# A hybrid decoder layer on one core: blocks of half-array products, ranks from backward schedules, a fixed opening and one engine for the norm

## The chip, the cores and the metric

The kernel runs on one core of one Trainium2 chip. The metric is the device time of one execution in microseconds (us); the figure compared is the median over several executions. The engines are called as in the profile: PE is TensorE (matmuls), PEld its weight loads, DVE is VectorE, ACT is ScalarE, POOL is GpSimd, and SP issues most of the DMA transfers.

## The reference

One pre-norm layer of a hybrid autoregressive decoder is computed for 1024 tokens of width 1024, in fp32:

```python
h = rms_norm(x, norm_in_g)
p = h @ w_in                                   # one projection for all three head groups
y_rwkv = rwkv7_group(p_rwkv, ...)              # 8 heads x 64, a delta-rule state scanned over time
y_nsa  = nsa_group(p_nsa, ...)                 # 4 heads: compressed, selected and window attention
kv = rms_norm(mem, mem_norm_g) @ w_mem_kv      # 256 memory tokens
y_mem  = memory_group(p_mem, mem_k, mem_v)     # 4 heads of cross-attention
x = x + concat(y_rwkv, y_nsa, y_mem) @ w_out
return rms_norm(x, norm_final_g)
```

With 16 blocks of 64 tokens and a top 16 of blocks, the selected branch attends to every block up to the token's own.

## The kernel before, in words

**Tiles.** The eight 128-token tiles of `x` are normed (`normed`), transposed on PE against an identity (`transposed`, lines 633 to 640) and kept as a high and a low fp32r half in two `H` tiles (`hT`). Every projection (`proj`) streams 512 columns of `hT` through a 128x128 weight tile three times (high x high, high x low, low x high); a weight tile is loaded into `wr`, rounded by ACT into `wh` and subtracted by POOL or DVE into `wl` (`split`, lines 569 to 571).

**Norm of a tile.** `normed` squares the tile on ACT (line 622), makes the factor on POOL (lines 623 and 566, into the small tile `ss`, of which there are two), and multiplies by factor and gain: POOL takes the first `X_POOL` = 192 columns in two multiplications (lines 627 and 628), DVE the other 832 in one (line 630). It is called for the eight tiles of `x` and, later, the two of `mem`.

**RWKV.** After the projections, `elementwise` (lines 868 to 949) prepares each pair of heads on DVE, ACT and POOL. `inverse` solves the 32x32 triangular systems: 31 steps of two DVE instructions each (lines 761 and 762), then a way through DRAM (`md`, `nd`, `st_d`) and 32x32 products on PE. There are two inverses, each for two pairs of heads. When both are through, `chunk` advances the state over 16 chunks of 64 tokens, one after the other, with products of 64 rows or 64 columns.

**Half-array products.** A product whose stationary operand has at most 64 (or 32) rows or columns uses a part of the 128x128 array; `_mode` gives its form as (rows, columns), each rounded up to 32, 64 or 128. They are emitted in groups without anything between them: 16, 8, 8 and 8 of them in a chunk, 32 in each of the four product steps of an inverse, 8 in each half of `elementwise`, 16 or 32 in the compression. An fp32 product shows as two matmul records in the trace.

**The order.** Every stage is a generator; `flow` interleaves them with ranks and latencies written by hand, and so emits one sequence of instructions. `ordered` then replaces this sequence. It reads the instructions, derives their dependences (`_depend`) and the reuse of buffers (`_slots`), and simulates the five engines with costs of its own (`_schedule`): whenever an engine is free, it takes of the instructions that are ready the one with the highest rank. The rank of an instruction is the length of the longest path of work behind it (`tail`), with engines taken as unlimited. PE lowers the rank of a candidate of another form than the last by `SWITCH` = 300 (ns). This is done in `ROUNDS` = 4 rounds, each from the order of the one before, and the order with the earliest simulated end is pinned on each engine:

```python
for a, b in zip(line, line[1:]):
    tc.add_manual_dep(ops[b].i, ops[a].i.name, ..., reason="order")
```

So each engine has one fixed order on the chip, and an instruction that isn't ready holds up all behind it on its engine.

Of the kernel before, what the change touches and what calls it, by code (L numbers as in the profile page):

```python
# [79 lines left out]
L_LAST = 1.41  # L80
L_W = 2.38
X_W = 1
X_POOL = 192
L_XW = 0.42
E_POOL = 1
E_KV = 0
# [194 lines left out]
def _depend(ops):  # L281

    past, bank = {}, {}
    for o in ops:
        o.data, o.same = set(), set()
        for t, parts in o.reads:
            for q, m in parts.items():
                for e in past.get((t.name, q), ()):
                    if e[0] & m and (e[2] or t.space == PSUM and ops[e[1]].e != o.e):
                        o.data.add(e[1])  # L290
        for t, parts in o.writes:
            for q, m in parts.items():
                keep = []
                for e in past.get((t.name, q), ()):
                    if e[0] & m:
                        o.data.add(e[1])
                        e = (e[0] & ~m, e[1], e[2])
                    if e[0]:
                        keep.append(e)
                keep.append((m, o.k, True))  # L300
                past[t.name, q] = keep
        for t, parts in o.reads:
            for q, m in parts.items():
                past.setdefault((t.name, q), []).append((m, o.k, False))
        if o.e == "PE":
            t = o.writes[0][0].name
            if t in bank:
                o.same.add(bank[t])
            bank[t] = o.k
        o.data.discard(o.k)  # L310
        if o.e == "PE":
            o.same |= {p for p in o.data if ops[p].e == "PE"}
            o.data -= o.same
# [29 lines left out]
    return took, late  # L343


def _schedule(ops, users, tags, took, phase, rank=None):
    n = len(ops)
    preds = [None] * n
    for o in ops:
        preds[o.k] = {p: 0 for p in o.data}  # L350
        for p in o.same:
            preds[o.k][p] = 1
    for names in tags.values():
        for a, b in zip(names, names[1:]):
            p = users[a][0]
            for k in users[b]:
                if k != p and any(w[0].name == b for w in ops[k].writes):
                    preds[k].setdefault(p, 2)
    for t, old in took.items():

        for k in users[t]:
            if any(w[0].name == t for w in ops[k].writes):
                for p in users[old]:
                    if p != k:
                        preds[k][p] = 1 if ops[k].e == "PE" and ops[p].e == "PE" else 0
    for o in ops:
        o.preds = preds[o.k]
    succ = [[] for _ in range(n)]
    for k in range(n):
        for p, same in preds[k].items():  # L370
            succ[p].append((k, same))

    deg = [len(s) for s in succ]
    tail = [0.0] * n
    stack = [k for k in range(n) if not deg[k]]
    seen = 0
    while stack:
        k = stack.pop()
        seen += 1
        o = ops[k]  # L380
        t = o.took
        for s, same in succ[k]:
            t = max(t, (0.0 if same == 2 else o.occ if same else o.took + LAG[ops[s].e]) + tail[s])
        tail[k] = t
        for p in preds[k]:
            deg[p] -= 1
            if not deg[p]:
                stack.append(p)
    assert seen == n, "a circle"
    if rank is not None:  # L390
        tail = [tail[k] + rank(ops[k]) for k in range(n)]
    indeg = [len(p) for p in preds]
    ready = [700.0] * n
    engines = ("PE", "DVE", "Activation", "Pool", "SP")
    free = dict.fromkeys(engines, 700.0)
    wait = {e: [] for e in engines}
    able = {e: [] for e in engines}
    order = {e: [] for e in engines}
    start = [0.0] * n
    for o in ops:  # L400
        if not indeg[o.k]:
            heapq.heappush(wait[o.e], (ready[o.k], o.k))
    lanes, port, holder, server = [0.0] * LANES, 0.0, "", 0.0
    slow, busy, prev, pe_at, pe_occ = True, 0.0, None, 0.0, 0.0
    done, end = 0, 0.0
    while done < n:
        best = None
        for e in engines:
            w, a = wait[e], able[e]
            while w and w[0][0] <= free[e]:  # L410
                k = heapq.heappop(w)[1]
                heapq.heappush(a, (-tail[k], k))
            at = free[e] if a else w[0][0] if w else None
            if at is not None and (best is None or at < best[0]):
                best = at, e
        at, e = best
        if not able[e]:
            free[e] = at
            continue
        if e == "PE" and prev is not None and len(able[e]) > 1:  # L420
            a = able[e]
            m = _mode(prev)
            k = min(a, key=lambda x: (x[0] + SWITCH * (_mode(ops[x[1]].shape) != m), x[1]))
            a.remove(k)
            heapq.heapify(a)
            k = k[1]
        else:
            k = heapq.heappop(able[e])[1]
        o = ops[k]
        s = at  # L430
        if e == "PE":

            if prev is not None and _mode(o.shape) != _mode(prev) and s < pe_at + pe_occ + 100:
                s = max(s, pe_at + pe_occ + 100 * (1 + slow))
            if prev is not None:
                a1 = min(s, pe_at + pe_occ)
                w0 = int((pe_at + phase) // WINDOW)
                e1 = (w0 + 1) * WINDOW - phase
                busy += min(a1, e1) - pe_at
                w1 = int((s + phase) // WINDOW)  # L440
                if w1 > w0:
                    slow = busy < 0.5 * WINDOW or slow and busy < 0.8 * WINDOW
                    busy = max(0.0, a1 - e1)
                    if w1 > w0 + 1:
                        slow, busy = slow or busy < 0.5 * WINDOW or w1 > w0 + 2, 0.0
            pe_at, prev = s, o.shape
            pe_occ = o.occ * (1 + slow)
            free[e] = s + pe_occ
            f = s + o.took * (1.5 if slow else 1.0)
        elif o.dma:  # L450
            issue, l0, serve, l1 = o.dma
            lane = min(range(LANES), key=lambda x: lanes[x])
            s = max(s, lanes[lane])
            server = max(server, s + issue + l0) + serve
            f = server + l1
            lanes[lane] = f
            free[e] = s + o.occ
        else:
            t, c = o.took, o.occ
            if o.lock:  # L460
                x = max(0.0, port - s) if holder != e else 0.0
                t, c, port, holder = t + x, c + x, s + t + x - 30, e
            f = s + t
            free[e] = s + c
        start[k] = s
        order[e].append(k)
        done += 1
        end = max(end, f)
        for x, same in succ[k]:
            ready[x] = max(ready[x], s if same == 2 else free[e] if same else f + LAG[ops[x].e])  # L470
            indeg[x] -= 1
            if not indeg[x]:
                heapq.heappush(wait[ops[x].e], (ready[x], x))
    return order, start, end


SWITCH = 300.0
BUFS = {"A_a": N_A, "C_a": 2, "P4_p4": N_P4, "NP_p4": N_NP, "S2_s2": N_S2, "N2_s2": N_N2, "T2_s2": N_T2, "H_h": 2, "wr_w": N_WR,
        "wl_w": 2, "wh_w": 2, "pa_ps": 6, "ch_ps": 2, "ss_small": 2, "edge_small": 2, "n8_small": 2, "ost_small": 2, "mst_small": 4,
        "cst_small": 1, "st_small": 2, "wst_small": 3, "xe_small": 1, "sgc_small": 1, "md_dram": 2, "nd_dram": 2}  # L480
ROUNDS = 4


def ordered(nc, tc, log=None):
    ops = _read(list(nc.cur_bb.bb.instructions))
    _depend(ops)
    users, tags = _tiles(ops)
    seq = list(range(len(ops)))
    best = None
    for n in range(ROUNDS):  # L490
        took, late = _slots(users, tags, seq)
        order, start, end = _schedule(ops, users, tags, took, 1100.0)
        if log is not None:
            log(n, late, end)
        if best is None or end < best[0]:
            best = end, order
        seq = sorted(range(len(ops)), key=lambda k: (start[k], k))
    end, order = best
    for e, line in order.items():
        for a, b in zip(line, line[1:]):  # L500
            tc.add_manual_dep(ops[b].i, ops[a].i.name, mybir.DependencyInfo(mybir.DependencyClass.NoSync, mybir.DependencyReason.DATA), reason="order")
# [1337 lines left out]
```

## Time and profile before

| | |
|---|---|
| median of three runs | 833.57 us (832.88 to 837.31) |
| profiled execution, its own time | 830.76 us |
| its span, first to last instruction | 829.0 us |
| mean granted TensorE clock | 0.968 |
| PE busy | 768.8 us, 93% of the span |
| PEld, DVE, ACT, POOL busy | 620.0, 537.3, 386.6, 362.0 us |
| HBM | 126 GB/s over the span |

The span is what the profiler sees of the program's instructions; the execution's own time is 1.8 us longer, and the median of the timed runs is 2.8 us above that execution. Busy time of PE is the union of its matmuls, whose ends are modelled, so a busy PE may still advance slowly: at a low clock, or between two products of different forms. The granted clock tells the first, start-to-start distances of consecutive matmuls the second.

### The profile page before, as it was taken

What the parts mean: (1) busy time and instruction counts of PE and PEld (TensorE: products, weight loads), DVE (VectorE), ACT (ScalarE), POOL (GpSimd) and SP (SyncE); (2) the same over time, 40 slices, a digit from 0 to 9 for tenths busy, and PEclk for the clock granted to TensorE, in tenths of its full rate; (3) what the DMA queues carried; (4) which work ended last, traced back from release to release, by engine and by line L of the source; (5) the groups of instructions that cost most, each with busy time, mean ns of one, the idle gap of its engine ahead of it and who ended that gap; (6) DMA issues with size and microseconds to landing.
All of it is one profiled execution on the core that took longest, in us unless ns stands there. A gap on an engine that the chain in (4) does not pass through costs nothing.

```text
span 829.0 us, 15125 instructions
## 1 busy us (share of the span) xinstructions
PE 768.8 (93%) x5738; PEld 620.0 (75%) x5738; DVE 537.3 (65%) x1044; ACT 386.6 (47%) x854; POOL 362.0 (44%) x390
## 2 busy tenths in 40 slices
PE   1999999999897799899999999999998999999996
PEld 0978778787676578678787667776787988888884
DVE  4753647749987529734578786646978776776542
ACT  4542516244153113333377653435477756665541
POOL 5644716346145010513446356625424153255664
PEclk9999899999988699999999999999999999999998
DMA  8011444665437992697556575632424020221121
GB/s 339 27 44 34 138 90 132 161 158 147 114 77 202 186 202 91 172 178 211 168 173 204 167 254 182 205 96 84 127 92 157 8 66 19 71 77 51 52 84 57
DMA packets 124745, 105.67 MB, mean 127 GB/s; under 512 B 50817, under 2 KB 108545, under 8 KB 122497
## 3 DMA queue, kind: packets, MB, share of 16 engines
q1 hardware_dynamic: 108096, 95.57, 41.4%
q10 hardware_dynamic: 16576, 9.14, 4.2%
q8 instruction: 45, 0.74, 0.3%
q14 instruction: 28, 0.22, 0.1%
HBM read 68.52 MB, written 36.18 MB: 126 GB/s over the span
## 4 chain that ended last, share of the span: by engine, by line
PE 71%; DVE 12%; DMA 6%; ACT 4%; issue 3%; POOL 3%; SPq 1%; ACTq 0%; DVEq 0%; POOLq 0%
PE pa L545 42%; PE ch L545 21%; PE pa L1571 3%; DVE P L761 2%; POOL wl L571 2%; DVE A L762 2%; DMA A<-st_d 1%; DMA wr<-in_w_in_dram 1%; DMA pv<-in_pv_dram 1%; DMA g_d<-T 1%; PE pa L1154 1%; PE pa L1603 1%; ACT wh L570 1%; DMA C<-st_d 1%; DVE C L942 1%
## 5 line engine op out<-in xcount | busy, mean ns | idle before, releaser
L545 PE MATMUL pa<-H,wh 128*128 128x512 f32 (+1 forms) x928 | 294.8, 406 | 1.3 <-ACT H L639 0.8
L545 PEld LDWEIGHTS pa<-H,wh 128*128 128x128 f32 x928 | 174.6, 195 | 38.2 <-issue 3.1
L545 PE MATMUL pa<-H,wl 128*128 128x512 f32 (+1 forms) x464 | 170.7, 400 | 0.0
L571 POOL TENSOR_TENSOR wl<-wr,wh 128x1024 fp32r<-128x1024 f32 x27 | 67.6, 2503 | 100.9 <-ACT wh L570 86.2
L545 PE MATMUL ch<-H,C 128*128 128x512 f32 x360 | 109.9, 410 | 0.6 <-DVE P L1691 0.5
L545 PEld LDWEIGHTS pa<-H,wl 128*128 128x128 f32 x464 | 89.3, 193 | 16.9 <-issue 0.7
L545 PE MATMUL pa<-A 128*128 128x256 f32 (+4 forms) x416 | 87.6, 313 | 4.4 <-DVE A L925 2.0
L570 ACT ACTIVATE wh<-wr 128x1024 fp32r<-128x1024 f32 x32 | 33.9, 1058 | 103.6 <-PE pa L545 82.9
L545 PEld LDWEIGHTS ch<-H,C 128*128 128x128 f32 x360 | 63.9, 189 | 10.2 <-DVE P L1691 0.9
L545 PEld LDWEIGHTS pa<-A 128*128 128x128 f32 (+1 forms) x416 | 55.1, 173 | 14.4 <-issue 3.8
L1531 DVE TENSOR_REDUCE wst<-pa 128x1 f32<-128x384 f32 (+3 forms) x96 | 46.5, 518 | 20.8 <-PE pa L545 20.4
L545 PEld LDWEIGHTS ch<-T,C 128*64 128x64 f32 (+1 forms) x1008 | 39.3, 136 | 22.9 <-issue 8.1
L545 PE MATMUL ch<-T,C 128*64 128x64 f32 (+1 forms) x1008 | 51.8, 231 | 4.0 <-issue 1.5
L1106 DVE TENSOR_TENSOR N<-pa,S 128x512 fp32r<-128x512 f32 (+1 forms) x76 | 45.3, 614 | 9.1 <-ACT S L1105 4.3
L1105 ACT ACTIVATE S<-pa 128x512 fp32r<-128x512 f32 (+1 forms) x76 | 39.7, 546 | 14.5 <-PE pa L1571 13.3
L1541 ACT ACTIVATE NP<-pa,wst 128x384 f32<-128x384 f32 (+3 forms) x52 | 29.0, 566 | 28.8 <-DVE wst L1537 18.1
L1428 DVE SCALAR_TENSOR_TENSOR T<-ch,gc,sgc 64x64 f32<-64x64 f32 x120 | 33.9, 283 | 11.7 <-PE ch L545 5.2
L761 DVE TENSOR_TENSOR P<-A 128x31 f32<-128x31 f32 (+15 forms) x62 | 31.2, 504 | 10.7 <-DMA g_d<-T 9.5
L545 PE MATMUL ch<-N,A 128*128 128x256 f32 x132 | 35.5, 320 | 1.4 <-DVE N L1106 1.4
L545 PE MATMUL ch<-S,A 128*128 128x256 f32 x132 | 35.3, 317 | 1.1 <-ACT T L1584 1.1
L1612 POOL TENSOR_TENSOR S<-S,N 128x512 f32<-128x512 f32 x8 | 10.3, 1287 | 59.2 <-DVE N L1611 52.0
L1410 POOL TENSOR_TENSOR sgc<-T,gc 64x256 f32<-64x256 f32 x30 | 20.4, 680 | 35.8 <-DVE T L1428 34.6
(277 smaller groups left out, 1587.6 us busy)
## 6 DMA issues: line engine op xcount, KB each, us to landing
C<-st_d SPq DMA_DIRECT2D x16, 1024.0 KB, 6.1
wr<-in_w_in_dram SPq DMA_DIRECT2D x28, 512.0 KB, 3.9
st_d<-C SPq DMA_DIRECT2D x32, 256.0 KB, 4.0
st_d<-A SPq DMA_DIRECT2D x24, 256.0 KB, 4.4
A<-in_x_dram SPq DMA_DIRECT2D x8, 512.0 KB, 7.8
st_d<-NP SPq DMA_DIRECT2D x8, 512.0 KB, 3.4
P<-in_x_dram SPq DMA_DIRECT2D x8, 512.0 KB, 3.5
out_dram<-P SPq DMA_DIRECT2D x7, 512.0 KB, 2.6
```

What stands on the lines that cost most here:

```text
L545: PE.matmul(o, l, r, start=start, stop=stop, skip_group_check=True, **k)
L570: S.activation(hi, src, AF.Copy)
L571: E.tensor_sub(lo, src, hi.bitcast(F32))
L761: V.tensor_mul(t3, mt[:, 0:n, s:s + 1].to_broadcast([128, n, m]), lt[:, s:s + 1, s + 1:].to_broadcast([128, n, m]))
L762: V.tensor_add(mt[:, 0:n, s + 1:], mt[:, 0:n, s + 1:], t3)
L1105: S.activation(th[:, 0:w], psum_t, AF.Copy)
L1106: V.tensor_sub(tl_[:, 0:w], psum_t, th[:, 0:w].bitcast(F32))
L1410: G.tensor_mul(sgc[r], sv[r, q], gcb[r])
L1428: V.scalar_tensor_tensor(svn[r, q, hp, :], pn[r, hp, :], g1[r, hp], sgc[r, hp, :], op0=OP.mult, op1=OP.add)
L1531: V.tensor_reduce(st[:, 3 + a, hh:hh + 1], sc[:, 0:cw], axis=AX.X, op=OP.max, negate=True)
L1541: S.activation(p[:, c0:c0 + cw], sc[:, 0:cw], AF.Exp, bias=m, accum_out=acc)
L1571: PE.transpose(pt[:, (2 * jj + hh) * 128:(2 * jj + hh + 1) * 128], ptl[hh][:, (j + jj) * 128:(j + jj + 1) * 128], ident)
```

## The change

Four things change, none of them in what is computed.

- `X_POOL` becomes 0: the two POOL multiplications of `normed` go, and DVE's one instruction covers all 1024 columns.
- Consecutive PE instructions of one form other than (128, 128) become a block of up to 32, which `_forward` issues without anything between; all that any member waits for is asked of the first. `SWITCH` becomes 700.
- The rank comes from `_backward`: the same list scheduling from the end of the program to its start, with one instruction at a time on each engine and the start times of the last round to choose by. An instruction's rank is its distance from the end in that schedule. There are 10 rounds in place of 4. The simulated clock counts products of 32 rows as half busy and those of 64 rows as 0.85.
- The first `FIRST` = 250 instructions of the emitted sequence get their rank raised, by 1000 for each place they stand ahead of the 250th, so that they keep about the order in which they were emitted.

Besides, two reads of one PSUM tile by the same engine now keep their order (`_depend`).

```diff
-X_POOL = 192
+X_POOL = 0
@@ _depend
-                    if e[0] & m and (e[2] or t.space == PSUM and ops[e[1]].e != o.e):
-                        o.data.add(e[1])
+                    if e[0] & m and (e[2] or t.space == PSUM):
+                        (o.data if e[2] or ops[e[1]].e != o.e else o.same).add(e[1])
@@ _edges (new; its first part is that of _schedule)
+    after, head = {}, list(range(len(ops)))
+    for a, b in zip(ops, ops[1:]):
+        if a.e == b.e == "PE" and _mode(a.shape) == _mode(b.shape) != (128, 128) and len(block(head, a.k, after)) < BLOCK:
+            after[a.k] = b.k
+            head[b.k] = head[a.k]
+    for k in range(len(ops)):
+        h = head[k]
+        if h != k:
+            for p, same in preds[k].items():
+                if head[p] != h:
+                    preds[h][p] = min(same, preds[h].get(p, 2))
@@ _backward (new), the core
+        k = heapq.heappop(able[e])[1]
+        o = ops[k]
+        R[k] = max(floor[k], at + o.occ)
+        free[e] = at + o.occ
+        for p, same in preds[k].items():
+            q = ops[p]
+            d = 0.0 if same == 2 else q.occ if same else q.took + LAG[o.e] + MARGIN
+            floor[p] = max(floor[p], R[k] + d)
@@ _forward (was _schedule)
+        if forced is not None:
+            k, e, at = forced, "PE", free["PE"]
...
         if e == "PE":
+            forced = after.get(k)
...
-                busy += min(a1, e1) - pe_at
+                share = 0.5 if prev[1] == 32 else 0.85 if prev[1] == 64 else 1.0
+                busy += (min(a1, e1) - pe_at) * share
@@ constants
-SWITCH = 300.0
+MARGIN = 0.0
+FIRST = 250
+BLOCK = 32
+SWITCH = 700.0
-ROUNDS = 4
+ROUNDS = 10
@@ ordered
-        order, start, end = _schedule(ops, users, tags, took, 1100.0)
+        preds, after = _edges(ops, users, tags, took)
+        rank = _backward(ops, preds, start)
+        rank = [r + max(0.0, FIRST - k) * 1e3 for k, r in enumerate(rank)]
+        order, start, end = _forward(ops, preds, after, rank, 1100.0)
```

## Rows read from the trace of the kernel before

**Rows 1.** The page: the span and the busy time of the engines.

```profile
span 829.0 us, 15125 instructions
PE 768.8 (93%) x5738; PEld 620.0 (75%) x5738; DVE 537.3 (65%) x1044; ACT 386.6 (47%) x854; POOL 362.0 (44%) x390
```

**Rows 2.** Windows by stage: stretch, length, busy (x instructions), clock, DMA share, GB/s.

```profile
42.46:220.00 177.54, 173.19 (x888) 138.44 (x887) 112.86 (x155) 66.37 (x101) 84.17 (x84) 0.98 0.46 114
220.00:380.00 160.00, 141.36 (x1109) 113.08 (x1108) 105.98 (x199) 49.92 (x76) 40.98 (x47) 0.88 0.69 155
380.00:545.00 165.00, 161.15 (x1749) 120.90 (x1747) 112.27 (x269) 90.75 (x223) 86.65 (x94) 1.00 0.61 192
545.00:640.00 95.00, 89.67 (x698) 70.36 (x699) 66.14 (x121) 52.04 (x113) 36.68 (x27) 0.98 0.39 118
640.00:820.94 180.94, 180.27 (x1139) 154.90 (x1137) 111.96 (x261) 103.48 (x302) 88.68 (x95) 1.00 0.16 53
```

**Rows 3.** Timeline of the opening: start, us, engine, line, instruction [idle before <-releaser].

```profile
8.28 0.54 POOL L566 TENSOR_TENSOR ss<-ss,der 128x1 f32<-128x1 f32 x1
10.19 1.08 DVE L630 SCALAR_TENSOR_TENSOR A<-A,ss,P 128x832 f32<-128x832 f32 x1
11.36 1.06 ACT L622 ACTIVATE S<-A 128x1024 bf16<-128x1024 f32 x1 [1.97 <-DVE A L630]
...
13.02 1.08 DVE L630 SCALAR_TENSOR_TENSOR A<-A,ss,P 128x832 f32<-128x832 f32 x1
13.23 1.26 POOL L566 TENSOR_TENSOR ss<-ss,der 128x1 f32<-128x1 f32 x1
...
16.60 1.38 POOL L628 TENSOR_TENSOR A<-A,P 128x192 f32<-128x192 f32 x1
...
18.03 1.33 PE L637 MATMUL ch<-cst,A 128*128 128x128 f32 x5 [18.03 <-POOL A L628]
```

**Rows 4.** Line 630 alone: its durations, ns, as least/median/most.

```profile
L630 DVE SCALAR_TENSOR_TENSOR A<-A,ss,P x8: 1077/1351/1542, 10.2 to 32.1; 128x832 f32<-128x832 f32 x8
```

**Rows 5.** The window from the first scaling to the last tile of `hT`.

```profile
10.19:40.16 29.97, 20.89 (x142) 20.02 (x143) 22.40 (x29) 17.39 (x31) 21.31 (x29) 1.00 0.42 155
```

**Rows 6.** Timeline of PE in a projection at the full clock.

```profile
56.17 1.07 PE L545 MATMUL pa<-H,wh 128*128 128x512 f32 x4
57.08 0.62 PE L545 MATMUL pa<-H,wl 128*128 128x512 f32 x2
```

**Rows 7.** Timeline of PE among the chunks.

```profile
443.52 0.39 PE L545 MATMUL pa<-N,P 128*128 128x512 f32 x1
443.84 0.33 PE L545 MATMUL ch<-T,C 64*64 64x64 f32 x2
444.09 0.39 PE L545 MATMUL pa<-A 128*128 128x256 f32 x1
...
444.69 1.06 PE L545 MATMUL ch<-T,C 64*64 64x64 f32 x22
445.68 0.50 PE L545 MATMUL pa<-N,P 128*128 128x512 f32 x1
```

**Rows 8.** Timeline of PE: the first and the last run of half-array products.

```profile
96.76 0.58 PE L545 MATMUL pa<-A,NP 64*128 64x128 f32 x1
...
591.09 0.33 PE L545 MATMUL pa<-kcs,NP 64*64 64x64 f32 x2
```

**Rows 9.** Timeline of PE about its two longest waits of the middle stage.

```profile
257.38 0.59 PE L545 MATMUL ch<-cst,A 128*128 128x2 f32 x2 [3.06 <-ACT NP L940]
...
259.55 1.22 PE L545 MATMUL pa<-H,wh 128*128 128x512 f32 x2
...
274.87 0.28 PE L545 MATMUL pa<-S,A 32*32 32x32 f32 x2 [4.17 <-DMA A<-st_d]
...
276.40 1.05 PE L545 MATMUL pa<-H,wh 128*128 128x512 f32 x2
```

**Rows 10.** Timeline of POOL: the weight split ahead of those products.

```profile
252.89 2.43 POOL L571 TENSOR_TENSOR wl<-wr,wh 128x1024 fp32r<-128x1024 f32 x1 [0.38 <-ACT wh L570]
```

More of the change, by code (lines that the diff above doesn't have):

```diff
@@ L310, in _depend @@
         o.data.discard(o.k)
+        o.same -= o.data | {o.k}
         if o.e == "PE":
@@ L343, in _slots, with _edges @@
     return took, late
-def _schedule(ops, users, tags, took, phase, rank=None):
-    n = len(ops)
-    preds = [None] * n
+def _edges(ops, users, tags, took):
+    preds = [None] * len(ops)
     for o in ops:
@@ L365, in _schedule, with block, _backward, _forward @@
                         preds[k][p] = 1 if ops[k].e == "PE" and ops[p].e == "PE" else 0
+    after, head = {}, list(range(len(ops)))
[9 more added lines that the diff above has]
+                    preds[h][p] = min(same, preds[h].get(p, 2))
     for o in ops:
         o.preds = preds[o.k]
+    return preds, after
+def block(head, k, after):
+    n, x = [], head[k]
+    while x is not None:
+        n.append(x)
+        x = after.get(x)
+    return n
+def _backward(ops, preds, first):
+    n = len(ops)
+    succ = [0] * n
+    for p in preds:
+        for k in p:
+            succ[k] += 1
+    R, floor = [0.0] * n, [0.0] * n
+    engines = ("PE", "DVE", "Activation", "Pool", "SP")
+    free = dict.fromkeys(engines, 0.0)
+    wait = {e: [] for e in engines}
+    able = {e: [] for e in engines}
+    for o in ops:
+        if not succ[o.k]:
+            heapq.heappush(wait[o.e], (0.0, o.k))
+    done = 0
+    while done < n:
+        best = None
+        for e in engines:
+            w, a = wait[e], able[e]
+            while w and w[0][0] <= free[e]:
+                k = heapq.heappop(w)[1]
+                heapq.heappush(a, (-first[k], k))
+            at = free[e] if a else w[0][0] if w else None
+            if at is not None and (best is None or at < best[0]):
+                best = at, e
+        at, e = best
+        if not able[e]:
+            free[e] = at
+            continue
+        k = heapq.heappop(able[e])[1]
+        o = ops[k]
+        R[k] = max(floor[k], at + o.occ)
+        free[e] = at + o.occ
+        done += 1
+        for p, same in preds[k].items():
+            q = ops[p]
+            d = 0.0 if same == 2 else q.occ if same else q.took + LAG[o.e] + MARGIN
+            floor[p] = max(floor[p], R[k] + d)
+            succ[p] -= 1
+            if not succ[p]:
+                heapq.heappush(wait[q.e], (max(0.0, floor[p] - q.occ), p))
+    return R
+def _forward(ops, preds, after, rank, phase):
+    n = len(ops)
     succ = [[] for _ in range(n)]
@@ L371, in _schedule @@
             succ[p].append((k, same))
[L373 to L391, printed above, removed]
     indeg = [len(p) for p in preds]
@@ L399, in _schedule @@
     start = [0.0] * n
+    member = set(after.values())
     for o in ops:
-        if not indeg[o.k]:
+        if not indeg[o.k] and o.k not in member:
             heapq.heappush(wait[o.e], (ready[o.k], o.k))
@@ L404, in _schedule @@
     slow, busy, prev, pe_at, pe_occ = True, 0.0, None, 0.0, 0.0
-    done, end = 0, 0.0
+    done, end, forced = 0, 0.0, None
     while done < n:
[L407 to L426, printed above, removed]
-        else:
-            k = heapq.heappop(able[e])[1]
+        if forced is not None:
+            k, e, at = forced, "PE", free["PE"]
+        else:
+            best = None
+            for e in engines:
+                w, a = wait[e], able[e]
+                while w and w[0][0] <= free[e]:
+                    k = heapq.heappop(w)[1]
+                    heapq.heappush(a, (-rank[k], k))
+                at = free[e] if a else w[0][0] if w else None
+                if at is not None and (best is None or at < best[0]):
+                    best = at, e
+            at, e = best
+            if not able[e]:
+                free[e] = at
+                continue
+            if e == "PE" and prev is not None and len(able[e]) > 1:
+                a = able[e]
+                m = _mode(prev)
+                k = min(a, key=lambda x: (x[0] + SWITCH * (_mode(ops[x[1]].shape) != m), x[1]))
+                a.remove(k)
+                heapq.heapify(a)
+                k = k[1]
+            else:
+                k = heapq.heappop(able[e])[1]
+        forced = None
         o = ops[k]
@@ L442, in _schedule @@
                     slow = busy < 0.5 * WINDOW or slow and busy < 0.8 * WINDOW
-                    busy = max(0.0, a1 - e1)
+                    busy = max(0.0, a1 - e1) * share
                     if w1 > w0 + 1:
@@ L469, in _schedule @@
         for x, same in succ[k]:
-            ready[x] = max(ready[x], s if same == 2 else free[e] if same else f + LAG[ops[x].e])
+            ready[x] = max(ready[x], s if same == 2 else free[e] if same else f + LAG[ops[x].e] + MARGIN)
             indeg[x] -= 1
-            if not indeg[x]:
+            if not indeg[x] and x not in member:
                 heapq.heappush(wait[ops[x].e], (ready[x], x))
     return order, start, end
-SWITCH = 300.0
+MARGIN = 0.0
+FIRST = 250
+BLOCK = 32
+SWITCH = 700.0
 BUFS = {"A_a": N_A, "C_a": 2, "P4_p4": N_P4, "NP_p4": N_NP, "S2_s2": N_S2, "N2_s2": N_N2, "T2_s2": N_T2, "H_h": 2, "wr_w": N_WR,
@@ L488, in ordered @@
     seq = list(range(len(ops)))
-    best = None
+    best, start = None, seq
     for n in range(ROUNDS):
         took, late = _slots(users, tags, seq)
-        order, start, end = _schedule(ops, users, tags, took, 1100.0)
+        preds, after = _edges(ops, users, tags, took)
+        rank = _backward(ops, preds, start)
+        rank = [r + max(0.0, FIRST - k) * 1e3 for k, r in enumerate(rank)]
+        order, start, end = _forward(ops, preds, after, rank, 1100.0)
         if log is not None:
```

## The prediction

> **What bounds the kernel now.** I read the page first, then the windows by stage, then the timeline where PE waits. The page: PE is busy 93% of the span and no other engine that computes over 65%, so PE is the engine to follow [rows 1]. The windows say where its other time is. It has no matmul for the first 18.03 us [rows 3] nor after 820.94, 8.06 us ahead of the end [rows 1, 2]. From 640 to 820.94 it is busy 180.27 of 180.94 us at full clock: another order has nothing to give there. The chunk stage (380 to 545) lacks 3.85 us, 42 to 220 lacks 4.35, 545 to 640 lacks 5.33. The stage from 220 to 380 stands out: 18.64 us without a matmul, and a granted clock of 0.88, a mean of the levels of 2.4 and 1.2 GHz, which over 160 us is 19.2 us of pulses withheld [rows 2]. So of 829 us, 18 at the head and up to 37.8 in that one stage are what another order can give back, beside what changes of form cost inside busy time.
>
> What ends PE's waits? The first matmul waits for POOL's second multiplication on tile 0 [rows 3]. In the stage, the two longest waits are 4.17 us for a DMA load of the inverse and 3.06 us for an ACT eviction; after either, PE soon runs projection products (`pa<-H,wh`) [rows 9], whose weights POOL had split by 255.32 [rows 10]. So from 270.7 to 274.87 PE had products that it could have run, and stood in its fixed order before one that it could not; of the wait before 257.38 the last 2.06 us are of that kind. These 6.2 us are the price of order alone.
>
> **The change, part by part.**
>
> *DVE alone scales.* Gone are two POOL instructions for each of ten tiles. At the head the factor of tile 0 was ready at 8.28 + 0.54 = 8.82 and DVE's 832 columns at 11.27, but POOL's line 628 ran only from 16.60 to 17.98, and PE began at 18.03 [rows 3]. With 1024 columns on DVE at the least rate seen (1077 ns for 832, so 1326) tile 0 is whole at 11.5, at the median (1351, so 1663) at 11.9 [rows 4]. PE can begin at about 11.8, 6.2 us earlier: the upper bound. The opening, however, is not over when PE starts but when the last tile of `hT` is there, at 40.16, and on that way DVE is the fullest engine: 22.40 of 29.97 us, idle for 7.57 [rows 5]. A tile costs DVE between 0.02 us less (1326 for 1351) and 0.31 more; I take 0.1, since POOL's long instructions beside it go and the small ones stay: 8 x 0.1 = 0.8. If half of the idle time goes with the earlier start, 3.8 - 0.8 = **3.0 us** come off. If it all stays, because the square of a tile waits for one of the two `ss` (ACT at 11.36 waits for DVE on tile 0 [rows 3]), the head loses 2.5 (8 x 0.31): the lower bound. The two `mem` tiles are covered by PE's other products; without that cover they cost 2 x 0.31.
>
> The same rows hold something against it: the power on POOL (line 566) takes 0.54 us alone and 1.26 with DVE's scaling beside it [rows 3], and the scaling grows by a fourth. The Trainium skill, "SBUF — State Buffer", section "Who interferes with whom", says that a VectorE instruction with two SBUF inputs and a GpSimd instruction that reads SBUF exclude each other for the whole instruction. By that rule each of eight tiles pays the 0.72 us between those two rows, half of it in the path as two tiles are under way: 2.9 us, and the head gives nothing. By the rows the second tiles pay it already, and POOL's long readers go; I keep 3.0.
>
> *The first 250 in their emitted order.* By the code these are the constants, three norms, nearly all transposes and the first projection. On SP the first weight tile then goes third instead of sixth, ahead of tiles 2 to 4 of `x`. The third square was held until 11.36 anyway, after 1.97 us of idle time on ACT [rows 3], which covers it; without that cover the late load costs what it exceeds that by. This part makes the 3.0 possible and has no term of its own.
>
> *Blocks.* Two full-array products of 512 columns start (57.08 - 56.17) / 4 = 0.23 us apart [rows 6]; ahead of a 64x64 product it is 0.32 (443.52 to 443.84). A lone pair of records then takes 0.25 to the next full-array product, while 22 in one run take 0.99, or 0.09 a pair [rows 7]. So cutting a run in two costs 0.09 + 0.16 = 0.25 us. Counted in time order, the 2302 half-array records from the first to the last run stand in 137 runs with 252 changes of form [rows 8]. By the code there are 97 blocks: 63 in the chunks, 8 in the inverses, 16 in `elementwise`, 10 in the rest. If each stands alone, 40 cuts go, 10 us: the upper bound; if the runs that now join several kinds fall apart, nothing. With `SWITCH` at 700 joins should stay; I take 30 cuts at 0.2, **6 us**. The price is a wait: the first of a block waits for what any member needs, and all behind it in PE's order too. In the chunks all members need the same few evictions, so I take nothing. In the inverses they wait for loads by DMA; that is a rival below. The kept order of two reads of a PSUM tile can delay one eviction by another on engines busy 65% or less [rows 1]; I take nothing.
>
> *Backward ranks.* The old rank is the longest path, blind to engines being taken; the new one is a place in a schedule with one instruction at a time. In 220 to 380 that should put products that are ready ahead of those that wait for the inverse. I count the 6.2 us of order alone, and a part of the low clock: after the wait at 257.38 two 512-column products take 1.22 us, where four take 1.07 at the full clock [rows 6, 9]. Of the 19.2 us withheld I take a fifth, 3.8. Sum **10 us**. Bounds: nothing, if waits as long arise elsewhere in the stage; 37.8, if all goes. Against it stand a new order's own misses, since waits such as those of rows 9 are what the planner did not foresee. The three stages about this one lack 13.5 us in all now; I add 30%, **4 us**.
>
> **Sum.** -3 - 6 - 10 + 4 = -15 us on 830.76, the profiled execution's own time, gives 815.8. The median of the runs stands 2.8 above that execution; -15 on 833.57 gives **818 us**. Half a per cent, 4.2 us, is about what a measurement here can tell from no change.
>
> **The rivals.**
> - *The stage fills.* Half of the 37.8 us comes back and no new misses arise: -3 - 6 - 18.9 = -28, 805 us. For it: PE had products ready in its longest waits. Against: DVE, which feeds most of PE's products there, is itself busy for 105.98 of the 160 us [rows 2].
> - *Only the small parts arrive.* The stage's waits move and stay as long: -3 - 6 + 4 = -5, 828 us.
> - *No change.* The planner keeps the best of ten orders by its own clock, and that need not be the chip's best: misses of 9 us (two waits like that of 4.17) take back head and blocks. 833 us.
> - *Slower: blocks held by DMA.* Each inverse has two groups of operands that come back through DRAM, so four blocks can stand in PE's order ahead of a load. One does now: 4.17 us, with a low clock behind it. Priced with the 3.8 us above as well, such a wait costs 8. Three more: -9 + 24 = +15, 849 us. It decides from the second on. For it: the first of 32 members now waits for all loads. Against: the loads of a group are issued together.
>
> **How the numbers follow.** The forecast 0.50, the stage fills 0.15, only the small parts 0.14, no change 0.08, slower 0.13. The prediction is the likeliest, 818; its own range is 811 (head and blocks at their upper bounds, 6.2 and 10) to 824 (the blocks at nothing). The range takes in all but the slower rival and a stage that fills further: 802 to 840, which leaves out about 0.16. Faster by over 0.5%: 0.50 + 0.15 + 0.14, less a little for 828 near the edge, 0.77; within it 0.09; slower 0.14.
>
> **What would show it.** Right: PE's first matmul near 12 us, no line 628, the last `hT` tile near 37; under 110 runs of half-array products; in the stage ahead of the first chunk under 12 us without a matmul and a clock over 0.92; the last 180 us as now. Wrong: a first matmul near 12 with `hT` still at 40 (head); blocks that wait for `A<-st_d` or `A<-md` (the slower rival); PE idle for longer in the stages about (misses).

## The result, and the profile after

The changed kernel takes **801.43 us** (median of 4 runs, 798.56 to 804.46) against 833.23 for the kernel before: a ratio of 0.9612, 95% interval [0.9562, 0.9661]. That is 32 us, twice the 15 forecast, and 0.6 us below the low end of the range. Between the two profiled executions the span falls from 829.0 to 800.1 us, 28.9 us; the account below is of these.

The page's head, the lines that answer to [rows 1], and the slices of the granted clock:

```profile
span 800.1 us, 15116 instructions
PE 730.0 (91%) x5738; PEld 599.8 (75%) x5738; DVE 531.3 (66%) x1044; ACT 387.8 (48%) x854; POOL 349.4 (44%) x370
PEclk9999999999995699898999999999999999999999
```

PE is busy for 38.8 us less than before with the same 5738 matmuls: what went is time inside busy PE. The share of the span fell too, so there is more waiting than before. The windows by stage, columns as in [rows 2]:

```profile
42.46:220.00 177.54, 175.41 (x984) 145.26 (x983) 120.71 (x176) 76.16 (x118) 89.45 (x95) 1.00 0.52 130
220.00:380.00 160.00, 127.26 (x1156) 105.14 (x1155) 93.59 (x190) 44.37 (x70) 32.14 (x35) 0.85 0.69 162
380.00:545.00 165.00, 158.44 (x1901) 121.86 (x1901) 120.12 (x275) 95.56 (x235) 94.16 (x100) 1.00 0.59 187
545.00:640.00 95.00, 88.90 (x576) 72.06 (x574) 77.42 (x155) 61.76 (x146) 32.32 (x24) 1.00 0.31 89
640.00:793.00 153.00, 152.94 (x952) 131.32 (x950) 89.69 (x207) 84.96 (x245) 82.86 (x89) 1.00 0.18 61
```

Ahead of 545 PE issues more matmuls in the same time (984 for 888, 1156 for 1109, 1901 for 1749), and what is left for the full stretch at the end takes 153 us in place of 181. The stage from 220 to 380 went the other way from the forecast: 32.74 us without a matmul for 18.64, a clock of 0.85 for 0.88. PE's timeline there, and all engines in the twenty microseconds about the wait (columns as in [rows 2]):

```profile
242.35 1.06 PE L1004 MATMUL ch<-cst,NP 128*128 128x128 f32 x8 [2.90 <-DVE NP L984]
260.21 0.28 PE L610 MATMUL pa<-S,A 32*32 32x32 f32 x2 [16.80 <-DMA A<-st_d]
262.89 3.59 PE L610 MATMUL pa<-S,A 32*32 32x32 f32 x126 [2.40 <-DMA S<-nd]
266.41 0.80 PE L610 MATMUL pa<-S,BO 128*128 128x512 f32 x1
```

```profile
240.00:260.00 20.00, 1.06 (x8) 0.86 (x8) 9.17 (x23) 4.34 (x6) 0.18 (x1) 0.58 0.91 189
```

PE stands for 16.80 us before the first block of the inverse, whose operands come by DMA. This is the place that the slower rival named: the wait came once, twice as long as the 8 us that it was priced at, and the total fell all the same. That the blocks make it, as the rival had it, is not what the experiments show (see the wait at the inverse below). The clock of 0.58 in this window costs little, since PE has nothing to run in it.

The opening, for [rows 3 to 5] (timeline of POOL, DVE and PE; line 695 alone; the window from 10.19, as in [rows 5], to the end of PE's wait for the last tile of `hT`):

```profile
8.13 0.55 POOL L631 TENSOR_TENSOR ss<-ss,der 128x1 f32<-128x1 f32 x1
...
10.10 1.28 DVE L695 SCALAR_TENSOR_TENSOR A<-A,ss,P 128x1024 f32<-128x1024 f32 x1
...
11.44 1.97 PE L702 MATMUL pa<-cst,A 128*128 128x128 f32 x8 [11.44 <-DVE A L695]
...
12.91 1.28 DVE L695 SCALAR_TENSOR_TENSOR A<-A,ss,P 128x1024 f32<-128x1024 f32 x1
13.12 1.47 POOL L631 TENSOR_TENSOR ss<-ss,der 128x1 f32<-128x1 f32 x1
...
39.61 0.39 PE L610 MATMUL pa<-H,wh 128*128 128x256 f32 x1 [2.21 <-DVE H L705]
```

```profile
L695 DVE SCALAR_TENSOR_TENSOR A<-A,ss,P x8: 1272/1278/1284, 10.1 to 29.5; 128x1024 f32<-128x1024 f32 x8
```

```profile
10.19:39.61 29.42, 24.15 (x161) 21.52 (x162) 26.39 (x33) 18.85 (x33) 15.48 (x17) 1.00 0.42 158
```

The first matmul starts 6.6 us earlier, but the last tile of `hT` is there at 39.6, only half a microsecond earlier. ACT and DVE ahead of it:

```profile
32.46 1.08 ACT L704 ACTIVATE H<-ch 128x512 fp32r<-128x512 f32 x2 [2.32 <-PE ch L702]
...
36.08 2.76 DVE L897 TENSOR_TENSOR A<-S,A 64x512 fp32r<-64x512 f32 x1
38.87 0.69 DVE L705 TENSOR_TENSOR H<-ch,H 128x512 fp32r<-128x512 f32 x1
```

ACT has its half of the tile ready at 33.54. DVE's subtraction (line 705) stands in DVE's fixed order behind four instructions of other work, from 34.45 to 38.84, of which line 897 alone takes 2.76 us.

**An account of PE's time.** Every distance from one matmul's start to the next is put under one head: the idle time that the timeline shows ahead of the second; else, the step of a half-array record; else, that of a full-array one. A half-array record is one of the 2302 of [rows 8], and a run is a stretch of them of one form. The steps add up to the start of the last matmul, in us:

| | before | after | difference |
|---|---|---|---|
| up to the first matmul | 18.0 | 11.4 | -6.6 |
| waits of PE behind it | 34.1 | 51.6 | +17.5 |
| steps of half-array records | 108.9 | 87.8 | -21.1 |
| steps of full-array records | 659.5 | 641.9 | -17.6 |
| start of the last matmul | 820.5 | 792.7 | -27.8 |

Of the 17.6 in full-array steps, 8.5 are the low clock (7.0 for 15.5 us: half of the time that these steps spend at the lower of the two granted levels), 4.4 the steps that lead into a run of half-array records (8.7 for 13.1 above a step within full-array work), and 4.7 the pace of the rest. So the half-array runs with their entries gave 21.1 + 4.4 = 25.5 us, the largest part of the gain; the 17.5 us of new waits take back nearly what the first matmul, the clock and the pace give.

### The profile page after: what moved, and what is told of

The parts are those of the page before. It is cut to its first block, busy times and chain, and to the rows that moved or that the text cites. A ratio compares the mean times of both kernels' runs of the same rounds, so it can differ in the third digit from the quotient of the medians.

```text
span 800.1 us, 15116 instructions
## 1 busy us (share of the span) xinstructions
PE 730.0 (91%) x5738; PEld 599.8 (75%) x5738; DVE 531.3 (66%) x1044; ACT 387.8 (48%) x854; POOL 349.4 (44%) x370
## 5 line engine op out<-in xcount | busy, mean ns | idle before, releaser
L610 PEld LDWEIGHTS pa<-H,wh 128*128 128x128 f32 x928 | 170.9, 191 | 40.0 <-DVE H L705 4.0
L610 PE MATMUL pa<-H,wl 128*128 128x512 f32 (+1 forms) x464 | 181.1, 391 | 0.3 <-DVE wl L636 0.3
L610 PE MATMUL ch<-H,C 128*128 128x512 f32 x360 | 100.6, 407 | 0.0
L610 PE MATMUL pa<-A 128*128 128x256 f32 (+4 forms) x416 | 75.1, 306 | 2.5 <-DVE A L897 2.1
L610 PEld LDWEIGHTS pa<-A 128*128 128x128 f32 (+1 forms) x416 | 51.1, 173 | 8.1 <-issue 2.5
L1171 DVE TENSOR_TENSOR N<-pa,S 128x512 fp32r<-128x512 f32 (+1 forms) x76 | 44.8, 613 | 17.8 <-ACT S L1170 15.2
L610 PEld LDWEIGHTS ch<-T,C 128*64 128x64 f32 (+1 forms) x1008 | 35.1, 139 | 22.1 <-ACT T L1483 5.7
L610 PE MATMUL ch<-T,C 128*64 128x64 f32 (+1 forms) x1008 | 42.1, 230 | 8.8 <-DMA C<-st_d 3.1
L1170 ACT ACTIVATE S<-pa 128x512 fp32r<-128x512 f32 (+1 forms) x76 | 38.5, 542 | 16.7 <-PE pa L1636 15.9
L876 ACT ACTIVATE T<-pa,pv 128x512 f32<-128x512 f32 x34 | 23.1, 679 | 32.4 <-PE pa L610 28.3
L1606 ACT ACTIVATE NP<-pa,wst 128x384 f32<-128x384 f32 (+3 forms) x52 | 29.0, 565 | 17.6 <-DVE wst L1596 11.1
L1677 POOL TENSOR_TENSOR S<-S,N 128x512 f32<-128x512 f32 x8 | 10.3, 1290 | 50.3 <-DVE N L1676 22.0
L610 PE MATMUL ch<-S,A 128*128 128x256 f32 x132 | 30.9, 298 | 0.8 <-ACT S L1170 0.8
L610 PE MATMUL ch<-N,A 128*128 128x256 f32 x132 | 30.4, 297 | 1.0 <-DVE N L1171 1.0
```

The source lines that it names most:

```text
L610: PE.matmul(o, l, r, start=start, stop=stop, skip_group_check=True, **k)
L876: S.activation(t[:, 4:516], o, AF.Identity, scale=col(C_MU + idx))
L1170: S.activation(th[:, 0:w], psum_t, AF.Copy)
L1171: V.tensor_sub(tl_[:, 0:w], psum_t, th[:, 0:w].bitcast(F32))
L1606: S.activation(p[:, c0:c0 + cw], sc[:, 0:cw], AF.Exp, bias=m, accum_out=acc)
L1677: G.tensor_add(bo[0], bo[0], bo[1])
```

## The experiments

The ratios below are to the kernel before, run on the same chip; a ratio difference of 0.01 is 8.3 us. Each line's "half-array" is the time of those records with their entries, 122.0 us in the kernel before in 137 runs, 96.5 in 87 runs in the changed one. "Low clock" is half of the time that all of PE's steps, half-array ones too, spend at the lower granted level; 21.9 us in the kernel before. The last four columns are read from one profiled execution of each kernel; that of ranks alone is 7.4 us above its median. The difference of two of the ratios has an interval of 0.006 to 0.009 to either side, 5 to 7 us.

| kernel | ratio, 95% interval | runs | half-array | PE's waits | low clock |
|---|---|---|---|---|---|
| changed | 0.9612 [0.9562, 0.9661] | 87 | 96.5 | 51.6 | 13.6 |
| blocks alone | 0.9826 [0.9758, 0.9893] | 89 | 97.8 | 48.6 | 16.5 |
| ranks alone | 0.983 [0.9755, 0.9905] | 117 | 111.7 | 52.4 | 23.3 |
| head alone | 0.9876 [0.9818, 0.9933] | 139 | 124.6 | 35.0 | 16.2 |
| changed, no blocks | 0.9827 [0.9771, 0.9884] | 117 | 112.9 | 48.1 | 15.3 |
| changed, old rank | 0.9728 [0.9658, 0.9797] | 89 | 94.2 | 50.2 | 18.7 |
| changed, no kept opening | 0.9584 [0.9523, 0.9644] | 87 | 95.8 | 48.7 | 13.8 |
| changed, POOL scales too | 0.9709 [0.9652, 0.9765] | 87 | 93.1 | 59.6 | 16.3 |
| changed, halves apart | 0.9692 [0.9656, 0.9728] | 87 | 103.8 | 47.0 | 16.7 |
| changed, `nd` by SP | 0.9746 [0.9708, 0.9784] | 88 | 94.0 | 57.5 | 17.3 |
| late inverse | 0.9508 [0.945, 0.9566] | 87 | 91.2 | 44.8 | 14.9 |
| late inverse, `nd` by SP | 0.9543 [0.951, 0.9577] | 92 | 94.2 | 37.8 | 14.2 |

**One part alone on the kernel before.** Three kernels with the new planner's code, in which all but one part is set as before.

```diff
 # in all three: SWITCH 300, shares 1.0, the reads of _depend as before
 # blocks alone: the old rank, X_POOL 192, FIRST 0, ROUNDS 4
+BLOCK = 32
 # ranks alone: BLOCK 1, X_POOL 192, FIRST 0
+        rank = _backward(ops, preds, start)
+ROUNDS = 10
 # head alone: the old rank, BLOCK 1, ROUNDS 4
-X_POOL = 192
+X_POOL = 0
+FIRST = 250
```

> The kernel before with blocks alone: old ranks, four rounds, SWITCH 300, no fixed opening, POOL's share of the norm kept. Theory A (a run of half-array products is worth far more than its cuts, since the two records of a product and neighbouring products overlap only inside a run): 20 to 25 us off, 808 to 813, and the products of elementwise (A,NP, 64x128) fall from 31.2 us busy to about 20. Theory B (my price of a cut was right and the time of these products fell because the new ranks moved them out of stretches at the low clock): 6 us off, about 827, and A,NP stays near 30.

> The kernel before with ranks from backward schedules alone, ten rounds, without blocks, with SWITCH 300, without the fixed opening, POOL's share kept. Theory A: what is left of 32 us after blocks (25) and head (6.6) is nothing, so 833 within 6. Theory B: the ranks carry the change, 15 to 20 us off, 813 to 818, with the busy time of the half-array products down by 15 or more.

> The kernel before with the opening alone: X_POOL 0 and FIRST 250, old ranks, no blocks. If what PE gains at its first matmul reaches the end whole, 6.6 us off, about 826.5; by my prediction 3.0 off, 830; if it is lost again at the stage ahead of the chunks, which waits for DVE and not for PE, nothing, 833. The first matmul stands near 11.4 us in each case.

Blocks alone are worth 1.7%, ranks alone 1.7%, the head alone 1.2%: 39 us as a sum where the whole gives 32. That difference is inside the intervals; the half-array work shows an overlap, since blocks and ranks take 24.2 and 10.3 us off it by themselves and 25.5 together. Of the 24.2 PE's waits, which grow by 14.5 with blocks alone, keep more than half. So theory A of that run holds for the half-array time and not for the total. The head alone gives 10 us, more than the 6.6 that was the most expected, though its interval holds 6.6 too: 6.5 by the first matmul and 5.7 by the low clock, less 2.6 of half-array time. The ranks do it without a block, and pay 18.3 in waits, most of it at the inverse (columns: waited for, us in total, times, longest):

```profile
PE pa L609 <- DMA A<-st_d: 26.7, 2, 19.8
PE pa L701 <- POOL A L692: 12.3, 1, 12.3
```

The second of these lines is the head. With POOL still scaling, the first matmul of this kernel stands at 12.3: it is the new order that brings POOL's multiplications forward, whatever `X_POOL` is.

**One part taken out of the changed kernel.**

```diff
 # no blocks
-BLOCK = 32
+BLOCK = 1
 # old rank (_longest holds the rank of before)
-        rank = _backward(ops, preds, start)
+        rank = _longest(ops, preds)
 # no kept opening
-FIRST = 250
+FIRST = 0
 # POOL scales too
-X_POOL = 0
+X_POOL = 192
```

> The changed kernel without blocks (BLOCK = 1), all else as changed. Theory A: 20 to 25 us more than the changed kernel, 821 to 826, with the runs of half-array products above 120. Theory B: 6 more, 807. By a third way the wait of 16.8 us ahead of the inverse, which the block must bear, shrinks without it and the time stays at 801.

> The changed kernel with the old rank, the longest path, in place of the backward schedule; blocks, opening, SWITCH 700, X_POOL 0 and ten rounds stay. If the ranks are worth what they are alone (14 to 15 us), 815; if their gain is the same as that of the blocks (both keep half-array products together), 803 or less: SWITCH 700 and blocks do it without them. By my prediction, 10 - 4 = 6 more, 807.

> The changed kernel with FIRST = 0. If the emitted order of the opening is what lets PE start at 11.4, the first matmul goes back towards 18 and the time to 806; if POOL's share alone held it, the first matmul stays near 12 and the time at 801 within 4.

> The changed kernel with X_POOL = 192 as before. If POOL's two multiplications are what PE waits for even in the emitted order, the first matmul comes at 12 to 14 us and each tile costs POOL 1.1 us more, 1 to 3 us in all, 802 to 805; if the delay to 18 was only the old order, 801 within 2.

Without blocks 0.0215 of the ratio is lost, 18 us, and 16.4 us of half-array time come back: less than the 20 to 25 of theory A, and three times the 6 of theory B. The old rank loses 0.0116, 10 us; the account shows 5.1 of it as low clock. The kept opening shows no worth: 0.9584 without it, first matmul at 11.5. With POOL scaling again the first matmul is earlier, at 10.46, but 8 us are lost in waits elsewhere, which neither way of its expectation has; so what DVE alone brings in this order is not the early first matmul.

**What a half-array step depends on.** The 64x128 products of `elementwise`, the costliest of these products one by one, fell most. PE's row of them before, after, and in the next experiment (busy us, mean ns of one | idle before):

```profile
L545 PE MATMUL pa<-A,NP 64*128 64x128 f32 x256 | 31.2, 316 | 0.1
```

```profile
L610 PE MATMUL pa<-A,NP 64*128 64x128 f32 x256 | 19.4, 296 | 0.2 <-DVE A L983 0.2
```

```profile
L610 PE MATMUL pa<-A,NP 64*128 64x128 f32 x256 | 27.6, 305 | 0.0
```

In the kernel's order two such products in a row use either the same half of the array's rows (partitions 0 to 63, or 64 to 127) or the two halves by turns. In the trace of before, at full clock, 30 steps that stay on one half have a median of 0.223 us from product to product, 56 that change have 0.112. They are emitted by turns; blocks keep that order, and the old planner did not: 40 of its steps stay on one half (30 at full clock, 10 at the lower level), none in the changed kernel. The experiment keeps the blocks and turns the loop round:

```diff
                 for c in range(4):
-                    for q in range(2):
+            # halves apart: q outside, c inside
+                for q in range(2):
+                    for c in range(4):
                         r = slice(64 * q, 64 * q + 64)
                         mm(pe[q][:, c, :], bk[r, 4 * d + c, :], xr[r, 4 * d + c, :])
```

> The changed kernel with one loop turned round: each block of eight 64x128 products of elementwise issues the four of one half of the array's rows and then the four of the other, in place of one half and the other by turns. Blocks, ranks and the rest stay, and PE's order is otherwise nearly the same. Theory, the halves: in the trace of before, two such products in a row on one half start 0.21 to 0.22 us apart (full clock), on the two halves by turns 0.11; 16 blocks x 6 steps x 0.10 = 10 us more PE time, the row of these 256 records from 19.4 us to about 29, and a total 6 to 10 us above the changed kernel, a ratio to the kernel before of 0.968 to 0.973 (the changed kernel has 0.961). Rival, the runs' length alone: what a block saves is the change of form at its two ends; then the row stays at 19.4 +- 1 and the ratio at 0.961.

The row rises from 19.4 to 27.6 us and the ratio by 0.008, 6.7 us. The first run of it, the same sixteen products, in the changed kernel and then with the halves apart:

```profile
88.45 2.06 PE L610 MATMUL pa<-A,NP 64*128 64x128 f32 x32
90.44 1.09 PE L1004 MATMUL ch<-cst,NP 128*128 128x128 f32 x8
```

```profile
88.64 2.82 PE L610 MATMUL pa<-A,NP 64*128 64x128 f32 x32
91.39 1.09 PE L1004 MATMUL ch<-cst,NP 128*128 128x128 f32 x8
```

1.99 us by turns, 2.75 apart. The run is as long and what follows it is the same, so the turns have a price of their own. For 64x64 products the same count gives 0.058 us (median) whether the half of the rows stays or changes; there the half of the columns can change while the rows stay, so this does not tell what staying on one part of the array costs them. The Trainium skill, "TensorEngine Tiling (Array Packing)", section "Key Properties", says that different tiles of the array can load weights and multiply in parallel; the trace of the 64x128 form agrees (0.112 for 0.223), and the page gives no price for staying on one tile.

**The wait at the inverse.** It comes with the new ranks, not with the blocks. PE's waits for `A<-st_d` without blocks, and with blocks alone (columns as above):

```profile
PE pa L610 <- DMA A<-st_d: 19.3, 1, 19.3
```

```profile
PE pa L632 <- DMA A<-st_d: 8.1, 2, 6.4
```

Ranks alone have one of 19.8, and the changed kernel with the old rank has none of this kind. So the third way of the kernel without blocks, in which the block must bear the wait, is ruled out.

By the planner's own edges, a PSUM bank of `pa` may be first written only after the bank allotted before it in emitted order has been. `L_BACK` = 4.1 is the time that `flow` leaves, as it emits, between the inverse's loads and its first product; so banks of products that were ready stood behind that product, and it stood behind the loads. If so, moving the inverse's place in emitted order, and nothing else, should take the wait away:

```diff
 # late inverse
-L_BACK = 4.1
+L_BACK = 18.0
```

> The changed kernel with one constant changed, L_BACK from 4.1 to 18: flow emits the inverse's products, and so allots their PSUM banks and S2 tiles, later. Theory C (the 16.8 us wait is one of allotment: the planner lets a tile of a pool be written only after the tile allotted before it has had its first use, so every product that needs a newer PSUM bank stands behind the inverse's first product, which waits for its DMA): the wait falls below 4 us and most of the low clock behind it goes, 10 to 20 us off, 782 to 791. Theory D (there is no other work at that point, or the DMA way itself sets the time): the wait moves with the inverse and stays, 801 within 4.

The ratio falls to 0.9508: 794.19 us, faster than the changed kernel, and short of the 782 to 791 that theory C expected. The row of the wait is gone; a wait of 11.46 us, for ACT, took its place. So the early place in emitted order and the new ranks make the wait together, and in the changed kernel either one put otherwise takes it away. Which tiles hold the ready products back, the PSUM banks or the inverse's other tiles allotted with them, is argued from the code and not shown. PE, then ACT at that time, in this kernel:

```profile
258.93 0.79 PE L610 MATMUL pa<-S,BO 128*128 128x512 f32 x1 [11.46 <-ACT S L955]
```

```profile
255.93 1.76 ACTq L841 DMA_DIRECT2D S<-nd  x3
257.73 0.63 ACT L1048 ACTIVATE S<-T 128x512 f32<-128x512 f32 x1 [5.31 <-issue]
257.78 0.58 ACTq L841 DMA_DIRECT2D S<-nd  x1
258.27 0.61 ACT L955 ACTIVATE S<-C 128x512 fp32r<-128x512 f32 x1
```

ACT computes nothing between 252.42 and 257.73: its next instruction in order issues a load of `nd`, which waits for `nd` to be stored. Two kernels issue these loads from SP, one with the early inverse and one with the late. Both stop at the second round of the planner, which by its simulated ends is the round that the kernels that they are compared with keep.

```diff
-                    nc.scalar.dma_start(ai[64 * q:64 * q + 32], nd[a, q].rearrange("c s t -> s c t"))
+                    nc.sync.dma_start(ai[64 * q:64 * q + 32], nd[a, q].rearrange("c s t -> s c t"))
-ROUNDS = 10
+ROUNDS = 2
```

> The changed kernel with the four loads of nd of each inverse issued by SP in place of ACT (and two rounds of planning, the second of which the changed kernel keeps as well). Theory: PE's wait of 16.8 us for the DMA into A comes from PE's own fixed order, the inverse's first block ahead of products whose PSUM banks were allotted after it; then the wait stays within 3 us and the ratio within 0.957 to 0.965. Rival: ACT, which stands behind those loads, feeds the way to them; then the wait falls by 5 us or more and the ratio to 0.955 or less.

> The kernel with L_BACK at 18 with the same move of the nd loads from ACT to SP. There ACT stands idle for 5.31 us while its loads wait for the store of nd, and PE waits 11.46 us for ACT's tile S behind them. Theory, ACT's queue is held by its loads: that wait falls to about 6 us or less, the total by 4 to 6 us, the ratio to the kernel before from 0.951 to 0.944 to 0.946. Rival, S is late by its own inputs: the wait stays near 11 and the ratio near 0.951. If SP, held in ACT's place, is late with weights, waits for wh or wl rise and the ratio does too.

The early one still has one wait of that length; the late one has lost its longest. PE in either:

```profile
263.84 0.28 PE L610 MATMUL pa<-S,A 32*32 32x32 f32 x2 [16.22 <-DMA S<-nd]
```

```profile
258.17 0.49 PE L610 MATMUL pa<-S,BO 128*128 128x512 f32 x1 [1.72 <-ACT S L955]
```

So in the early kernel the wait is there whichever engine issues the loads, as PE's own order has it; it came out slower than the changed kernel, with 5.9 us more waiting in all, and why is open. In the late one the 11.46 was ACT's held queue: it falls to 1.72, and PE's waits by 7.0 in all. The total did not follow: 0.9543 against 0.9508, two intervals that overlap, where a fall by 0.005 to 0.007 was expected. Half-array time rose by 3.0, with 5 runs more, and the other steps of full-array records by 4.8, in an order that differs in many places. What ended the wait is shown; that removing it must gain is not.

## Why the prediction was wrong

**Blocks: the step that failed.** Its term was 30 cuts x 0.2 = 6 us, with 40 x 0.25 = 10 as upper bound. Measured: 16.4 us of half-array time and 18 of the total when the blocks are taken out, 24.2 of half-array time when they are put in alone. The count was too low, 50 runs fewer (137 to 87) where 40 was the bound: each block was taken to stand alone, but they join (blocks alone take away 48 runs, ranks alone 20). And the price was too low. The 0.09 a pair of [rows 7] has the ends of the run of 22 in it; inside a run of the trace a 64x64 product takes 0.058, so by that row standing alone costs 0.09 + 0.25 - 0.06 = 0.28, not 0.25. Taken from step to step at the full clock, the ends of a run (0.11 at its entry, 0.05 more for its first product with 64 columns and 0.10 with 64x128, 0.10 more for its last) make 0.26 for 64x64 and 0.31 for 64x128. Summed over all runs of either trace, lone products among them, the ends are 39.3 us before and 22.6 after: 16.7 us, 0.33 for each of the 50 runs.

By difference it is 0.51 a run (25.5 / 50), with 0.50 for blocks alone (24.2 / 48) and 0.52 for ranks alone (10.3 / 20), so a run's ends are not all. Inside the runs, steps of 64x128 products that stay on one half were 2.9 us in the kernel before and none after. Another 4.4 us (7.0 before, 2.6 after) are waits that no idle time shows. DVE and PE in a run of the chunks, in the kernel before:

```profile
396.30 2.49 DVE L1428 SCALAR_TENSOR_TENSOR T<-ch,gc,sgc 64x64 f32<-64x64 f32 x8 [2.25 <-issue]
...
396.74 2.44 PE L545 MATMUL ch<-T,C 128*64 128x64 f32 x32
```

PE follows DVE's eight instructions, which start 0.31 us apart, two products at a time. Another run of 32 such records takes 1.15 us at 390.46, where nothing inside it holds them. These three parts make 24.0 of the 25.5; the rest is not assigned.

**The head** was right in direction. Forecast 3.0; PE is busy for 27.00 us of the first 42.46, where it was for 23.19, so 3.8 us more work is done in the opening. Alone it gave 10 us in the total, with 5.7 of low clock that the term does not have. The first matmul came at 11.44 (forecast "about 11.8"), since a tile took 1.28 us, less than the least rate that the sum had (1.33). But the sign that was named, the last tile of `hT` near 37, was wrong: it came at 39.6, held by what stands ahead of it in DVE's order, and the gain came about because PE ran more projection products on the tiles that it had (161 matmuls in the window for 142 [rows 5]). The power on POOL did take 1.47 us beside the scaling and 0.55 alone. That is what the Trainium skill's rule on the shared port says ("SBUF — State Buffer", "Who interferes with whom"); the trace agrees with the rule, and the head gained all the same. And the early first matmul does not need the part that was named for it: the head alone brings it to 11.5, but so do the ranks by themselves, to 12.3, and in the changed kernel with POOL scaling it is earlier still, at 10.46.

**The first 250** have no term, and none shows (0.9584 without them, inside the interval of 0.9612).

**The stage** was put at -10 by the ranks: it was not to lose its waits. They grew from 18.64 to 32.74 us in the window. The ranks' 10 us in the total (old rank put back) agrees with the term by luck: about half of it is the low clock, 5.1 us, and the two waits that were counted did not go; the ranks put the longest one there.

**The misses** were put at +4. PE's waits grew by 17.5, and those for `A<-st_d` alone from 5.2 to 16.8. The slower rival had named the place. Three things it had wrong. It laid the wait to the blocks, and it is there without them (19.3, and 19.8 with ranks alone). Its price was that of the one wait seen before [rows 9], but such a wait lasts as long as the chain that it stands for, and 16.8 is two of its 8. And by its sum two such waits eat up head and blocks, put at 9 us together; these gave 3.8 in the opening and 16 to 18, and the total fell with the wait in it.

**Of the signs**: first matmul, line 628 and the runs (87, under 110) came as said, and the last stretch is full as before (152.94 of 153.00 us); `hT`, the stage's waits (under 12) and its clock (over 0.92) did not. The ten rounds have no run of their own; by its simulated ends the planner kept the second, which four would have reached too.

The range missed because its low end was made of the same block term: with 18 in place of 6 the forecast's own sum gives -27, 806 us, well inside it. That this comes so near is luck in part: the stage's waits and the misses went the wrong way, and the head and the clock gave more.

## What to carry to other kernels

Count changes of a PE array's form before and after a reordering and price them by the whole run, entry, first and last product, in each form that is there. Then look inside the runs, for the order of row halves and for waits that show as longer steps and not as idle time: here the ends of a run were 0.33 us where 0.2 was taken, and the gain was 0.51 for each run that went. Where a fixed order puts a group that waits for a load ahead of ready work, look for what forces it there (here, by the planner's edges, the order in which buffers are allotted) and move the group in the emitted order: one constant gave a further 1%. And a DMA that waits for data can hold up the compute of the engine that issues it (5.31 us of ACT here), so look at who stands behind it; that an emptied wait shortens the total has then still to be measured.

## What was not expected of the hardware

- fp32 products of 64 rows and 128 columns start 0.112 us apart when they use the two halves of the array's rows by turns, and 0.22 apart on one half; 64x64 products show 0.058 either way.
- The ends of a run of half-array products cost 0.26 us (64x64) to 0.31 us (64x128, by turns) at the full clock; by difference each run that went saved 0.50 to 0.52 us, in three kernels with 87, 89 and 117 runs, since waits and the order of halves inside the runs changed with it.
- A run of 128x64 products that follows DVE's instructions 0.31 us apart took 2.44 us in place of 1.15, and PE shows as busy throughout.
- DVE's scaling of 1024 columns took 1.27 to 1.28 us in all eight tiles, where 832 columns had taken from 1.08 to 1.54 beside POOL's share of it [rows 4].
